# First dense block of a hybrid decoder layer, taken whole or in two halves of its inputs

## The chip, the cores and the metric

The kernel runs on one core of a Trainium2 chip. The metric is the device time of one execution in microseconds (us). Engines are named as in the profile: PE is TensorE's matmul, PEld its weight load, DVE is VectorE, ACT is ScalarE, POOL is GpSimd, SP is SyncE, which here issues the DMAs.

## What is computed

One layer of a conditioned decoder in float32, for a prompt of 2048 rows and for 64 sample rows, both 1024 wide. Cut to what matters here:

```
mod = silu(c) @ w_ada + b_ada               # 9 rows x 6144: sh1, sc1, gt1, sh2, sc2, gt2
h   = rms_norm(x, norm1_g) * (1 + sc1) + sh1
q, k, v, g, u, gate_r, gate_s = split(h @ w_in)
ret = retention(rotary(q), rotary(k), v);  ssm = s5(u)      # S5: a diagonal state space model
x   = x + gt1 * (merge of both branches by the gates) @ w_out
x   = x + gt2 * squared_relu_mlp(rms_norm(x) * (1 + sc2) + sh2)
```

The first four of the twelve 512-column pieces of `mod` are sh1 (pieces 0 and 1) and sc1 (pieces 2 and 3). Pieces 0 and 2 are all that the first 512 columns of h need, pieces 1 and 3 what the other 512 need.

## The kernel before

The prompt goes through the dense part in four super-blocks of 512 rows, and then through the feed-forward part. In a super-block, `block()` computes one 512-column piece of a dense product: u, q, k, v, g, four gate pieces, then glu, br, bs and wo. In the first super-block a further piece of the modulation (`ada4` to `ada11`) follows each of the first eight.

Float32 operands are split into a rounded high part and a rest, both of the type fp32r, and a product is three matmuls: high by high, high by rest, rest by high. The weights come as a stream of pieces of 256 rows by 512 columns (512 KB). `fetch` (line 181) loads one into a buffer `wraw` (four of them). `refill` splits it into `whi` on ACT (line 191) and `wlo` on POOL, or on DVE for the modulation's weights (line 194), and then fetches another. The split pieces lie in a ring of five. For block u four pieces (u in `for u in range(nu)`) of two 128-row steps each meet four groups of 128 output columns: 4 x 2 x 4 x 3 = 96 matmuls (line 253), which gather in four banks of PSUM. Pieces 0 and 1 meet only the first half of h (`hh[0]`, `hl[0]`), pieces 2 and 3 only the second (`hh[1]`, `hl[1]`).

`setup()` (from line 768) prepares the first super-block. It queues all loads on SP in this order: constants, the weights of modulation piece 0, the first two row blocks of x and the bias, the weights of piece 2, the other two row blocks, the weights of pieces 1 and 3, and four fetches of the stream. Then, for each half of the columns: the product of the shift piece (line 845), in the first half also the row norms of x on ACT and DVE (lines 639 to 644, 625 to 633, 860), the product of the scale piece, and for each of the four row blocks a turn on PE (line 852), scale and shift on DVE (`m`, line 685), the split into `hh` on ACT (line 687) and `hl` on POOL (line 688). So the products run in the order 0, 2, 1, 3. `mod_out` adds the bias (`mt`, line 878), turns the result (`ptm`, line 883) and copies it (line 884). Two refills stand between products 1 and 3, three more at the end.

`s5_setup` (from line 925) prepares the constants of S5, nearly all of it small operations on DVE, with loads on SP and some transposes on PE. It runs as a generator beside the blocks of the first super-block: `tick()`, called once for each piece and column group of a block, takes it a step further, and what is left after block k is written out at once (`finish`).

The order in the text is not the order on the engines. The context is built with `schedule_with_timeline_sim=True`: a planner lays the instructions of each engine's queue by a modelled timeline, and the engine then runs that queue as laid. `keep_in_program_order` (the refills of `setup`) pins an instruction behind what its engine was given before it. Tiles of one pool share its slots: 17 in the pool `units` for the large ones, and two PSUM pools of four banks each, `pd` for the blocks and `pm` for the rest.

Of the kernel before, what the change touches and what calls it, by code (L numbers as in the profile page):

```python
# [10 lines left out]
F32 = mybir.dt.float32  # L11
# [6 lines left out]
P = 128  # L18
# [7 lines left out]
RING, RAW = 5, 4  # L26
# [56 lines left out]
class Layer:  # L83
# [148 lines left out]
            del self.open_side[name]  # L232
            self.spawn(evac(st[0]))

    def block(self, name, kind, src, evac=None, sample=None, order="k"):
        nc = self.nc
        assert self.names[self.at] == name, (self.names[self.at], name)
        self.at += 1
        nu = 2 if name == "glu" or name[:2] in ("br", "bs") else 4
        nk = 2 * nu  # L240
        banks = [self.pd.tile([P, 512], F32, tag="pd", name=f"pd_{name}") for _ in range(4)] if kind else []
        sb = self.bank(f"ps_{name}", [P, 512]) if sample else None

        def products(k, j, w, kk):
            hi, lo = w
            xh, xl = src(k, j)
            if kind == "T":
                a = slice(j * P, j * P + P)
                mm = [(hi[:, kk, a], xh), (hi[:, kk, a], xl), (lo[:, kk, a], xh)]
            else:  # L250
                mm = [(xh, hi[:, kk]), (xh, lo[:, kk]), (xl, hi[:, kk])]
            for z, (a, b) in enumerate(mm):
                nc.tensor.matmul(banks[j], a, b, start=(k == 0 and z == 0), stop=(k == nk - 1 and z == 2))  # L253

        def sample_products(k, w, kk):
            st = sample[0](k)
            m = st.shape[-1]
            for z in range(2):
                nc.tensor.matmul(sb[:m], st, w[z][:, kk], start=(k == 0 and z == 0),
                                 stop=(k == nk - 1 and z == 1))  # L260

        if order == "k":
            for u in range(nu):
                w = self.weight(name)
                for j in range(4 if kind else 0):
                    for kk in range(2):
                        products(2 * u + kk, j, w, kk)
                    if u == nu - 1:
                        evac(j, banks[j])
                    if j == 0:  # L270
                        self.refills()
                    self.tick()
                if sample:
                    for kk in range(2):
                        sample_products(2 * u + kk, w, kk)
                    if u == nu - 1:
                        self.spawn(sample[1](sb))
                    if kind is None:
                        self.refills()
                        self.tick()  # L280
                self.due += 1
                self.side()
            return
        self.refills()
        ws = [self.weight(name) for u in range(nu)]
        for j in range(4):
            for u in range(nu):
                for kk in range(2):
                    products(2 * u + kk, j, ws[u], kk)
                if u == nu - 1:  # L290
                    evac(j, banks[j])
                self.tick()
                if j == 3 and not sample:
                    self.refill()
        if sample:
            for u in range(nu):
                for kk in range(2):
                    sample_products(2 * u + kk, ws[u], kk)
                self.tick()
                self.refill()  # L300
            return self.spawn(sample[1](sb))
# [466 lines left out]
    def setup(self):  # L768
# [28 lines left out]
        gn = self.work("gn", [16, P])  # L797
        dma(gn[0:8], i["norm1_g"].rearrange("o (k p) -> (o k) p", p=P))
        dma(gn[8:16], i["norm2_g"].rearrange("o (k p) -> (o k) p", p=P))
        wa = [self.unit("wa") for _ in range(8)]  # L800
        wv = i["w_ada"][0].rearrange("(k p) n -> p k n", p=P)

        def load(n):
            for a in range(2):
                dma(wa[2 * n + a], wv[:, 4 * a:4 * a + 4, 512 * n:512 * n + 512])

        xu = [self.unit("x0", shape=(P, 2, D)) for _ in range(2)]
# [5 lines left out]
        load(2)  # L813
        for j in range(2, 4):
            self.x_rows(xu[1][:, j - 2], 0, j)
        load(1)
        load(3)
        for _ in range(RAW):
            self.fetch()

        th = self.work("th", [9, D])
# [3 lines left out]
        pt = self.bank("pt", [P, 8, 9])  # L825
# [14 lines left out]
        x = [xu[j // 2][:, j % 2] for j in range(4)]  # L840

        def ada(n):
            pa = self.pd.tile([P, 512], F32, tag="pd", name=f"ps_ada{n}")
            for k in range(8):
                nc.tensor.matmul(pa[:9], z[:, k, 0:9], wa[2 * n + k // 4][:, k % 4], start=(k == 0), stop=(k == 7))
            self.mod_out(n, pa[0:9], ba[:, 512 * n:512 * n + 512])

        def turn(q, j):
            pt = self.bank("pt", [P, 4, P])
            for a in range(4):  # L850
                k = 4 * q + a
                nc.tensor.transpose(pt[:, a], x[j][:, k * P:k * P + P], self.ident)
            return pt

        for q in range(2):
            ada(q)
            if q == 0:
                for j in range(4):
                    r = self.now(self.row_rstd(x[j]))
                    V.tensor_scalar(x[j], x[j], r, None, op0=ALU.mult)  # L860
                pts = [turn(q, j) for j in range(4)]
            else:
                for _ in range(2):
                    self.refill(True)
            ada(2 + q)
            self.scales(2 + q)
            for j in range(4):
                pt = turn(q, j) if q else pts[j]
                self.norm_out(pt, q, self.s1[:, :, 0], self.modT[:, 0:8, 0], self.hh, self.hl, j, nc.gpsimd)
        for _ in range(RING - 2):  # L870
            self.refill(True)
        self.late_setup = self.s5_setup()
# [2 lines left out]
    def mod_out(self, n, p, bias):  # L875
        nc = self.nc
        t = self.work("mt", [9, 512])
        nc.vector.tensor_add(t, p, bias)
        if n in (4, 5, 10, 11):
            nc.sync.dma_start(self.modd[:, 512 * n:512 * n + 512], t)  # L880
        pt = self.pd.tile([P, 4, 9], F32, tag="pd", name="ptm")
        for a in range(4):
            nc.tensor.transpose(pt[:, a], t[:, a * P:a * P + P], self.ident[:9, :9])
        nc.vector.tensor_copy(self.modT[:, 4 * n:4 * n + 4], pt)
# [615 lines left out]
    def super_block(self, b, late):  # L1500
# [4 lines left out]
        hh, hl = self.hh, self.hl  # L1505
        srcT = lambda h, l: (lambda k, j: (h[k // 4][:, k % 4], l[k // 4][:, k % 4]))
# [8 lines left out]
        S = lambda st, ev: (lambda k: st[:, k], ev) if smp else None  # L1515
        hS = zS = None
        if smp:
            hS = self.hS
# [20 lines left out]
        nc.sync.dma_start(rot, self.i["rot"][b])  # L1539
        if b == 0:  # L1540
            s5 = self.spawn(self.late_setup, 2)
        self.block("u", "T", srcT(hh, hl), ev_u, S(hS, ev_us))
        if b:
            s5 = self.spawn(self.s5(b), 7)
        more_ada()
# [231 lines left out]
        order = "j" if b < NSB - 1 else "k"  # L1777
        self.block("wo0", "N", srcN(mh, ml), ev_wo(0), S(m2S, ev_woS(0)) if smp else None, order=order)
        f = self.block("wo1", "N", srcN(mh, ml), ev_wo(1), S(m2S, ev_woS(1)) if smp else None, order=order)
# [49 lines left out]
```

## Time and profile before

| | |
|---|---|
| median of 3 runs | 3114.01 us (3114.0 to 3119.35) |
| profiled execution | 3112.17 us |
| its span in the trace | 3110.3 us |
| busy share PE, DVE, POOL, ACT | 94%, 62%, 55%, 42% |
| mean granted TensorE clock | 0.965 |
| end of modulation product 3 | 57.99 us |
| block u on PE | 59.09 to 82.75 us |

Times are counted from the span's start. In a row of the timeline the first number is the start, the second the duration (of all where several are merged), then the engine, the line of the kernel, the operation, output and inputs, the count, and in brackets how long the engine had been idle and what released it. In a row of the groups, busy time and mean nanoseconds stand behind the count. In a row of the waits stand the total, how often, and the longest.

### The profile page before, as it was taken

The numbers are of one execution on the slowest core, as the hardware profiler recorded it, in microseconds if no ns is written. First come the engines' busy times: TensorE is split into PE (matmuls) and PEld (weight loads), VectorE is DVE, ScalarE is ACT, GpSimd is POOL, SyncE is SP. The second block draws the span as 40 slices with busy tenths as digits, with TensorE's granted clock in tenths as the row PEclk, the third lists the DMA queues.
The fourth block names the chain that finished last, engine by engine and source line by source line (L and its number), as shares of the span: only waits on it lengthen the run. The fifth ranks groups of instructions, "written<-read, shape, count | busy, mean of one in ns | idle before, by whom it ended". The sixth has DMA issues, their size and how long they took to land. (4 is left out here: it accounts for less than half of the span.)

```text
span 3110.3 us, 37430 instructions
## 1 busy us (share of the span) xinstructions
PE 2917.2 (94%) x13436; PEld 2381.2 (77%) x13436; DVE 1924.5 (62%) x3205; ACT 1319.7 (42%) x2060; POOL 1722.9 (55%) x1036
## 2 busy tenths in 40 slices
PE   7789999999998899999999989999999999998996
PEld 3567777888777778777788778887788788876885
DVE  5978675770576896467853556565555755554555
ACT  2232442222333234423234345556664555566643
POOL 2331464434354544556345576768778666688771
PEclk9889999999999899999899999999999999999998
DMA  8565445644345854458544455556545544466532
GB/s 226 157 194 204 133 129 150 180 123 118 83 121 164 263 172 123 138 141 250 183 129 152 147 198 174 197 180 210 182 156 181 195 163 149 153 217 224 188 129 95
DMA packets 336749, 518.62 MB, mean 167 GB/s; under 512 B 71462, under 2 KB 168246, under 8 KB 332459
## 3 DMA queue, kind: packets, MB, share of 16 engines
q1 hardware_dynamic: 336564, 516.23, 52.7%
q8 instruction: 106, 1.74, 0.2%
q14 instruction: 79, 0.65, 0.1%
HBM read 401.39 MB, written 114.78 MB: 166 GB/s over the span
## 5 line engine op out<-in xcount | busy, mean ns | idle before, releaser
L194 POOL TENSOR_TENSOR wlo<-wraw,whi 128x1024 fp32r<-128x1024 f32 x248 | 614.0, 2487 | 733.8 <-ACT whi L191 627.5
L191 ACT ACTIVATE whi<-wraw 128x1024 fp32r<-128x1024 f32 x312 | 324.5, 1057 | 629.8 <-PE pd_wo L253 61.8
L409 PE MATMUL pq_down<-shi,tw 128*128 128x512 f32 x1792 | 564.4, 394 | 20.6 <-DVE acc L469 9.8
L409 PE MATMUL pq_up<-shi,tw 128*128 128x512 f32 x1792 | 555.9, 390 | 12.8 <-ACT tw L310 7.1
L409 PEld LDWEIGHTS pq_down<-shi,tw 128*128 128x128 f32 x1792 | 338.9, 189 | 96.5 <-ACT acc L467 9.5
L409 PEld LDWEIGHTS pq_up<-shi,tw 128*128 128x128 f32 x1792 | 337.1, 188 | 85.7 <-ACT tw L310 8.3
L311 POOL TENSOR_TENSOR tw<-traw,tw 128x512 fp32r<-128x512 f32 x192 | 277.4, 1459 | 147.7 <-ACT tw L310 147.5
L409 PE MATMUL pq_down<-slo,tw 128*128 128x512 f32 x896 | 351.9, 393 | 0.9 <-DVE slo L382 0.9
L409 PE MATMUL pq_up<-slo,tw 128*128 128x512 f32 x896 | 349.1, 390 | 0.0
L469 DVE SCALAR_TENSOR_TENSOR acc<-pq_down,modT,acc 128x512 f32<-128x512 f32 x224 | 162.9, 746 | 108.6 <-PE pq_down L409 108.1
L396 ACT ACTIVATE shi<-sw 128x1024 fp32r<-128x1024 f32 x140 | 147.1, 1058 | 156.1 <-DMA sw<-sd 105.4
L409 PEld LDWEIGHTS pq_down<-slo,tw 128*128 128x128 f32 x896 | 169.8, 189 | 35.5 <-DVE slo L382 1.4
L409 PEld LDWEIGHTS pq_up<-slo,tw 128*128 128x128 f32 x896 | 168.7, 188 | 34.6
L382 DVE TENSOR_TENSOR slo<-sw,far 128x512 fp32r<-128x512 f32 x160 | 103.8, 683 | 115.1 <-ACT far L381 97.1
L310 ACT ACTIVATE tw<-traw 128x512 fp32r<-128x512 f32 x224 | 138.0, 625 | 55.7 <-PE pq_down L409 46.8
L419 ACT ACTIVATE aq<-pq_up 128x512 f32<-128x512 f32 x128 | 72.5, 592 | 191.0 <-PE pq_up L409 190.9
L401 DVE TENSOR_TENSOR slo<-sw,shi 128x1024 fp32r<-128x1024 f32 x60 | 105.7, 1781 | 66.9 <-ACT shi L396 63.2
L345 POOL TENSOR_TENSOR ts<-traw,ts 128x512 f32<-128x512 f32 x64 | 95.8, 1496 | 53.2 <-issue 50.5
L194 DVE TENSOR_TENSOR wlo<-wraw,whi 128x1024 fp32r<-128x1024 f32 x64 | 83.1, 1300 | 54.3 <-ACT whi L191 50.2
L310 ACT ACTIVATE tw<-ts 128x512 fp32r<-128x512 f32 x128 | 80.0, 626 | 86.0 <-PE pq_up L409 76.0
L345 POOL TENSOR_TENSOR ts<-traw 128x512 f32<-128x512 f32 x64 | 86.5, 1351 | 47.2 <-DMA traw<-in_w_up_dram 28.9
L447 DVE TENSOR_TENSOR sq<-aq 128x512 f32<-128x512 f32 x32 | 31.3, 979 | 131.0 <-ACT aq L424 131.0
(536 smaller groups left out, 6992.6 us busy)
## 6 DMA issues: line engine op xcount, KB each, us to landing
wraw<-in_w_in_dram SPq DMA_DIRECT2D x144, 512.0 KB
sw<-sd SPq DMA_DIRECT2D x112, 512.0 KB
s5p<-s5c SPq DMA_DIRECT2D x32, 1024.0 KB
traw<-in_w_up_dram SPq DMA_DIRECT2D x64, 512.0 KB
sd<-sq SPq DMA_DIRECT2D x32, 1024.0 KB
sd<-aq SPq DMA_DIRECT2D x32, 768.0 KB
traw<-in_w_down_dram SPq DMA_DIRECT2D x24, 1024.0 KB
wraw<-in_w_ada_dram SPq DMA_DIRECT2D x32, 512.0 KB
```

The lines of the kernel that those rows point to most:

```text
L191: a = nc.scalar.activation(hi, raw, AF.Copy)
L194: l = eng.tensor_sub(lo, raw, hi)
L310: self.nc.scalar.activation(t[:, 0], x, AF.Copy)
L311: eng.tensor_sub(t[:, 1], x, t[:, 0])
L345: G.tensor_sub(x[p], l, x[m] if isinstance(m, int) else m)
L382: self.nc.vector.tensor_sub(d, a, c)
L396: nc.scalar.activation(hi[:, a], t, AF.Copy)
L401: V.tensor_sub(lo[:, a], t, hi[:, a])
L409: self.nc.tensor.matmul(bank, w, x, start=(first and a == 0 and z == 0), stop=(a == 3 and z == 2), skip_group_check=True)
L419: copy = lambda d, b: nc.scalar.activation(d, b, AF.Copy)
L447: V.tensor_add(S[:, 0], A21, A22)
L469: V.scalar_tensor_tensor(d, b, g, d, op0=ALU.mult, op1=ALU.add)
```

## The change

`block()` gets a parameter `part`. With part 0 it takes only the first two pieces of u's weights and keeps the four banks; with part 1 it goes on in these banks with the other two, and only then are the results taken out. Part 0 is called in `setup()` at the end of the first half of the columns: between product 2 with its norm, and product 1. Part 1 stands where the whole block stood, in the first super-block alone; the others call the block whole.

The loads change their order: two fetches of the weight stream now come ahead of the weights of products 1 and 3, the other two behind them. Those weights and the last two fetches stand behind product 0 in the text. The two pinned refills move to the end of the first half of the columns. Since u holds all banks of `pd` from part 0 on, products 1 and 3 and their turned results take banks of `pm`. The tiles for the modulation weights are allocated when they are loaded, no longer all ahead.

```
-    def block(self, name, kind, src, evac=None, sample=None, order="k"):
+    def block(self, name, kind, src, evac=None, sample=None, order="k", part=None):
...
-        self.at += 1
+        if part != 0:
+            self.at += 1
...
-        banks = [self.pd.tile([P, 512], F32, tag="pd", name=f"pd_{name}") for _ in range(4)] if kind else []
+        if part == 1:
+            banks = self.held
+        else:
+            banks = [self.pd.tile([P, 512], F32, tag="pd", name=f"pd_{name}") for _ in range(4)] if kind else []
+            self.held = banks
...
-            for u in range(nu):
+            for u in range(nu) if part is None else range(2 * part, 2 * part + 2):
...
-        wa = [self.unit("wa") for _ in range(8)]
+        wa = {}
...
             for a in range(2):
+                wa[2 * n + a] = self.unit("wa")
                 dma(wa[2 * n + a], wv[:, 4 * a:4 * a + 4, 512 * n:512 * n + 512])
...
-        load(1)
-        load(3)
-        for _ in range(RAW):
+        for _ in range(2):
             self.fetch()
...
-            pa = self.pd.tile([P, 512], F32, tag="pd", name=f"ps_ada{n}")
+            pa = self.pm.tile([P, 512], F32, tag="pm", name=f"ps_ada{n}") if n % 2 else \
+                self.pd.tile([P, 512], F32, tag="pd", name=f"ps_ada{n}")
...
             ada(q)
             if q == 0:
+                load(1)
+                load(3)
+                for _ in range(RAW - 2):
+                    self.fetch()
                 for j in range(4):
...
-            else:
-                for _ in range(2):
-                    self.refill(True)
             ada(2 + q)
...
+            if q == 0:
+                for _ in range(2):
+                    self.refill(True)
+                hh, hl = self.hh, self.hl
+                self.block("u", "T", lambda k, j: (hh[k // 4][:, k % 4], hl[k // 4][:, k % 4]), part=0)
...
-        pt = self.pd.tile([P, 4, 9], F32, tag="pd", name="ptm")
+        pool = ("pm", self.pm) if n % 2 else ("pd", self.pd)
+        pt = pool[1].tile([P, 4, 9], F32, tag=pool[0], name="ptm")
...
-        self.block("u", "T", srcT(hh, hl), ev_u, S(hS, ev_us))
+        self.block("u", "T", srcT(hh, hl), ev_u, S(hS, ev_us), part=None if b else 1)
```

## The prediction

> **What bounds the kernel now.** First the page, its totals and its slices.
>
> ```profile
> span 3110.3 us, 37430 instructions
> PE 2917.2 (94%) x13436; PEld 2381.2 (77%) x13436; DVE 1924.5 (62%) x3205; ACT 1319.7 (42%) x2060; POOL 1722.9 (55%) x1036
> PE   7789999999998899999999989999999999998996
> DVE  5978675770576896467853556565555755554555
> ```
>
> PE is busy for 94% of the span, so it sets the length over the whole. The exception is the first three slices (78 us each), the only early stretch where its digit falls to 7 and 8, and the change lies in the first. There I read the windows.
>
> ```profile
> 9.86:59.09 49.23, 38.66 (x112) 10.70 (x112) 18.69 (x66) 10.00 (x23) 9.69 (x6) 0.93 0.89 253
> 30.00:40.00 10.00, 6.18 (x22) 1.88 (x21) 5.34 (x25) 2.67 (x8) 0.00 (x0) 0.88 0.96 295
> 50.00:60.00 10.00, 9.22 (x32) 3.17 (x33) 1.98 (x7) 2.47 (x3) 6.54 (x4) 1.00 0.66 221
> 59.09:82.75 23.66, 23.66 (x108) 18.95 (x107) 22.90 (x77) 11.04 (x15) 9.84 (x6) 1.00 0.77 170
> 82.75:207.00 124.25, 94.37 (x419) 72.95 (x418) 121.91 (x243) 33.68 (x41) 47.43 (x21) 0.89 0.52 166
> ```
>
> The columns are the stretch, its length, then busy time of PE, PEld, DVE, ACT and POOL, the granted clock, the DMA share and GB/s. Until 59 us the DMA engines are busy for 0.89 and PE idles 49.23 - 38.66 = 10.6 us. Block u runs from 59.09 to 82.75 with PE full. Then, until 207 us, DVE is full (121.91 of 124.25) and PE idles 29.9 us. The waits from 60 to 260 us name who holds PE:
>
> ```profile
> PE pd_k L253 <- DVE rt L1553: 10.2, 1, 10.2
> PE pw L1151 <- DVE s5bx L1144: 8.0, 1, 8.0
> PE pt L909 <- DVE mt L903: 7.7, 1, 7.7
> PE pd_v L253 <- DVE rt L1553: 3.6, 1, 3.6
> ```
>
> All four are DVE. It works through the S5 setup from about 65 us, so from u on what counts is when DVE's stream starts and how fast it runs, not when PE finishes u. The timeline shows how that start comes about.
>
> ```profile
> 24.38 8.47 PE L845 MATMUL ps_ada<-wa,z 128*9 128x512 f32 x16 [4.43 <-DMA wa<-in_w_ada_dram]
> 38.32 8.32 PE L845 MATMUL ps_ada<-wa,z 128*9 128x512 f32 x16 [2.15 <-DMA wa<-in_w_ada_dram]
> 43.97 0.75 DVE L860 TENSOR_SCALAR x<-x,y 128x1024 f32<-128x1024 f32 x1
> 46.57 1.97 PE L852 MATMUL pt<-cpk,x 128*128 128x128 f32 x16
> 50.95 7.04 PE L845 MATMUL ps_ada<-wa,z 128*9 128x512 f32 x16
> 59.09 0.50 PE L253 MATMUL pd_u<-hh,whi 128*128 128x512 f32 x1
> 59.95 5.21 DVE L685 TENSOR_SCALAR m<-pt,s,modT 128x128 f32<-128x128 f32 x16
> 62.07 5.13 POOL L688 TENSOR_TENSOR hl<-m,hh 128x512 fp32r<-128x512 f32 x4 [5.54 <-ACT hh L687]
> 65.06 0.90 DVE L978 TENSOR_SCALAR s5w<-s5w 128x32 f32<-128x32 f32 x1
> 65.20 0.63 ACT L687 ACTIVATE hh<-m 128x512 fp32r<-128x512 f32 x1 [0.65 <-DVE m L685]
> 67.17 4.75 POOL L194 TENSOR_TENSOR wlo<-wraw,whi 128x1024 fp32r<-128x1024 f32 x2
> 82.75 0.39 PE L259 MATMUL ps_ada<-whi,cT 128*41 128x512 f32 x1
> ```
>
> The modulation products run in the order 0, 2, 1, 3 (24.38 is product 2, 38.32 product 1, 50.95 product 3, which ends at 57.99). Product 3 releases the second norm half: DVE 59.95 to 65.16, last hh at 65.83, last hl at 67.20. Today the first half of u already runs under that work, which is the cover that the change takes away.
>
> **The change part by part.** Every operation is kept; 48 of u's 96 products, two weight loads and two weight splits move. What it costs depends on three arrivals.
>
> ```profile
> 18.11 15.70 SPq L805 DMA_DIRECT2D wa<-in_w_ada_dram  x4
> 33.85 7.81 SPq L181 DMA_DIRECT2D wraw<-in_w_in_dram  x4
> 41.19 2.54 POOL L688 TENSOR_TENSOR hl<-m,hh 128x512 fp32r<-128x512 f32 x2 [40.75 <-ACT hh L687]
> 51.88 4.65 POOL L194 TENSOR_TENSOR wlo<-wraw,whi 128x1024 fp32r<-128x1024 f32 x2
> 54.27 2.67 SPq L181 DMA_DIRECT2D wraw<-in_w_ada_dram  x2
> 58.88 0.42 SPq L944 DMA_DIRECT2D s5w<-in_ssm_log_dt_dram  x1
> ```
>
> (a) SP. Two weight pieces (512 KB each, 1.05 MB) move ahead of the four 1 MB loads for products 1 and 3. At the 295 GB/s of the 30 to 40 us row that is 3.6 us: product 1 starts at about 38.3 + 3.6 = 41.9 instead of 38.32. By the row of the whole stretch (253 GB/s) it is 4.2 us. It ends 8.25 us later, at 50.1.
>
> (b) When the half block can start. The fourth row block of x is scaled at 44.7 (43.97 + 0.75). A turn is a third of the 1.97 us burst (0.7), the four DVE operations are a quarter of 5.21 (1.3), hh takes 0.63, hl half of 2.54 (1.3) and the pinned first wlo half of 4.65 (2.3). That gives 44.7 + 0.7 + 1.3 + 0.6 + 1.3 + 2.3 = 50.9. So the half block cannot fill the gap in front of product 1; PE gets to it after product 1, at 50.1 to 50.9.
>
> (c) PE. Half of 23.66 us is at most 11.8; 96 products without the setup's transposes between them are nearer 22, so 11.0. The half block runs from 51 to 62. It stands ahead of product 3 in the program, so product 3 runs from 62 to 69: the release of the second norm half moves by 69.0 - 58.0 = +11.0 us. It is bounded by +3.6 (product 3 goes first, only the loads are late) and +20 (the half block goes before product 1 too).
>
> (d) DVE in the meantime. The raw buffers of the first two pieces now come free after wlo at 51 and 53.2 rather than 54.2 and 56.5, so the small S5 loads behind those fetches on SP are issued some 3 us earlier than 58.88. DVE then has the chain for dt to do, which needs nothing from product 3, in time that was idle (the 50 to 60 us row: DVE 1.98 of 10):
>
> ```profile
> L980 DVE CAST s5w<-s5w 128x32 int32<-128x32 f32 x1 | 2.3, 2326 | 0.0
> L981 DVE CAST s5w<-s5w 128x32 f32<-128x32 int32 x1 | 2.3, 2312 | 0.0
> L986 DVE SCALAR_TENSOR_TENSOR s5w<-s5w 128x32 f32<-128x32 f32 x11 | 2.0, 183 | 0.2
> L979 DVE TENSOR_SCALAR s5w<-s5w 128x32 f32<-128x32 f32 x1 | 1.3, 1258 | 0.0
> L978 DVE TENSOR_SCALAR s5w<-s5w 128x32 f32<-128x32 f32 x1 | 0.9, 895 | 0.0
> ```
>
> These are 2.3 + 2.3 + 2.0 + 1.3 + 0.9 = 8.8 us; seven more of this shape at 0.183 make it 10.1. Between 57 and 71 us all of it fits. But POOL's splits stand beside DVE here: operations of 0.18 us take 2.3 in 67.17 to 71.9. One such split (the fourth piece) still comes behind hl and will hold some other operation for 2.4 us. The credit is 10.1 - 2.4 = 7.7, bounded by 0 (the order written for DVE has the norm first, so DVE waits) and 10.1.
>
> [...]
>
> (e) PE behind u. The second half needs the last hh, which trails product 3 by 65.83 - 57.99 = 7.8 us. So it runs from 76.8 to 88.6, 5.9 us later than 82.75, after a gap of 7.8 us. What such a gap costs more is seen after the wait for L903:
>
> ```profile
> 101.83 0.59 PE L909 MATMUL pt<-cpk,mt 9*128 9x9 f32 x4 [7.69 <-DVE mt L903]
> 102.36 1.22 PE L253 MATMUL pd_q<-hh,wlo 128*128 128x512 f32 x2
> 105.88 0.40 PE L253 MATMUL pd_q<-hl,whi 128*128 128x512 f32 x1
> ```
>
> Eight products took 3.52 us, 0.44 each against 0.23 (22 us by 96): +1.7. PE is late by 7.6 us, and that same wait of 7.7 us covers it. If the cover is gone, the sum is +7.6. [...]
>
> (f) The rest. Products 1 and 3 take banks of the second pool, since u now holds all four of the first; the transposes of the second half then queue behind product 3. One is 0.7 us, and 1.9 us of mt, ptm and scales (57.99 to 59.95) run over it: 0, bounded by 2.6 for four. If slots are reused in the order they were taken, those of x and not of wa now come first, so the loads of the S5 matrices on SP may wait for these transposes; SP's fetches queue behind, and the weights in the ring feed PE meanwhile: 0, bounded by +4. Eight fewer ticks under u leave more of the setup for later: an order, no work, bounded by 3.6 either way (the smallest of the four waits).
>
> Sum: +11.0 - 7.7 = +3.3 us. The profiled execution took 3112.17 us (its span and 1.9 around it); the median is 3114.01. So 3115.5 against the profile, 3117.3 against the median.
>
> **The rivals.** *Product 3 first* (faster): the plan puts product 3 straight after product 1, at 50.1, and ends it at 57.1 to 58 because the turns now lie in the gap before product 1. The half block covers the norm as today, and dt's credit stays: -7.7, 3106.3. For it: its loads land early (issued by 33.8 today). Against: the half block stands first in the program and is nearly ready at 50. *Half block first* (slower): the plan puts it ahead of product 1 too. It waits for the hl and wlo chain until 51 whatever the loads do, ends at 62, product 1 at 70.3, product 3 and its hand-over at 78.3: +20.3 - 7.7 = +12.6, 3126.6. This decides once the plan has x ready before the loads of product 1. For it: program order, and the loads now come later. Against: in today's order the plan placed product 1 ahead of the last turns. *No change in effect*: product 3 keeps its place and DVE's order keeps the norm first; only part of the 3.6 us shows: +0 to +3.6, some 3115.8.
>
> **How the numbers follow.** Forecast 0.40, product 3 first 0.25, half block first 0.20, no effect 0.15. This kernel's measurements can tell 0.2%, 6.2 us, from no change. The forecast's own range is +0.9 to +11 (a credit of 10.1 at one end, none at the other); I put a quarter of it over +6.2, since the rows speak for a credit near 7.7. Slower: 0.20 + 0.10 = 0.30. Faster: 0.25. Within: 0.30 + 0.15 = 0.45. The range 3104 to 3128 holds the three priced cases with a little beyond the fast one.
>
> **What would show it.** (a) Product 1 starting at 41 to 43. (b, c) pd_u products in two groups, the first from about 51 to 62 between products 1 and 3, and product 3 ending near 69. (d) L978 before the second group of L685. (e) A PE gap of some 7 us in front of the second group, and the wait for L903 nearly gone; DVE still full until about 210. The forecast is wrong if product 3 ends before 60, if the half block starts before 45, or if DVE is not the engine that holds PE at 200 us.

## The result and the profile after

The changed kernel takes 3142.31 us (median of 6 runs, 3138.3 to 3145.8) against 3119.29 us of the kernel before measured beside it (6 runs, 3114.0 to 3126.75): a ratio of 1.0079, 95% interval 1.0061 to 1.0097. It is slower by some 24 us; the forecast was +3.3. Runs of the kernel before spread by 13 to 36 us between the lowest and the highest of a batch, so the times of the experiments come from several runs each. A place is read from one profile, and places scatter too. Two kernels below, e14 and e16, have the order of before on every engine until after the start of the S5 setup. Their product 1 starts at 40.6 and 41.9 us instead of 38.3, their first S5 operation at 66.1 and 68.7 instead of 65.1. In e16:

```profile
41.88 8.34 PE L845 MATMUL ps_ada<-wa,z 128*9 128x512 f32 x16 [2.13 <-DMA wa<-in_w_ada_dram]
```

So a difference of less than some 4 us between the places of two kernels says little by itself.

The totals of the page after, and its slices:

```profile
span 3144.0 us, 37436 instructions
PE 2928.8 (93%) x13436; PEld 2391.6 (76%) x13436; DVE 1925.6 (61%) x3205; ACT 1319.0 (42%) x2060; POOL 1717.6 (55%) x1036
PE   6779998999998889999899989999999999998996
DVE  3997755682484896376863455655656855554555
```

The work is the same (DVE 1925.6 us busy against 1924.5). DVE's first slice falls from 5 to 3, so DVE has lost time at the very start. The windows of after say where (columns as in the prediction):

```profile
50.00:80.00 30.00, 27.82 (x105) 14.04 (x103) 4.94 (x15) 3.95 (x6) 8.92 (x5) 0.98 0.60 133
82.43:235.00 152.57, 117.32 (x510) 92.13 (x510) 147.91 (x309) 42.84 (x55) 50.24 (x24) 0.86 0.47 151
```

The same two windows of before:

```profile
50.00:80.00 30.00, 29.22 (x122) 19.17 (x123) 21.51 (x69) 11.10 (x15) 16.38 (x10) 1.00 0.73 175
65.06:213.90 148.84, 118.96 (x536) 93.86 (x535) 143.33 (x310) 44.61 (x57) 54.29 (x25) 0.89 0.54 167
```

From 50 to 80 us DVE worked 4.94 us instead of 21.51. The second row of each fence runs from DVE's first operation on the dt chain to the end of the last `pw` transpose of the S5 setup on PE; I call it the S5 stream. It starts 17.4 us later (82.43 against 65.06), is 3.7 us longer and ends 21.1 us later (235.0 against 213.9). Those 21 us are still there at the end of the block glu (439.6 against 417.8), and they are the loss. The two profiled executions differ by another 12 us behind glu (2692.6 and 2704.4 us); the other kernels below, all with the same work there, take from 2684.4 (e12) to 2704.8 us (e10), so I count that as scatter.

The timeline of after shows why the stream starts late (lines of the changed kernel: L850 is the product, L895 `ptm`, L690 `m`, L990 the first operation of the dt chain):

```profile
47.19 1.09 PE L857 MATMUL pt<-cpk,x 128*128 128x128 f32 x4 [6.61 <-DVE x L869]
48.20 8.53 PE L850 MATMUL ps_ada<-wa,z 128*9 128x512 f32 x16
56.66 1.21 PE L258 MATMUL pd_u<-hh,whi 128*128 128x512 f32 x4
56.77 0.68 DVE L889 TENSOR_TENSOR mt<-ps_ada,ba 9x512 f32<-9x512 f32 x1 [7.09 <-PE ps_ada L850]
67.81 0.41 PE L895 MATMUL ptm<-cpk,mt 9*128 9x9 f32 x4
68.15 7.04 PE L850 MATMUL ps_ada<-wa,z 128*9 128x512 f32 x16
68.25 0.33 SPq L953 DMA_DIRECT2D lam<-in_ssm_lambda_re_dram  x1
70.02 0.42 SPq L956 DMA_DIRECT2D s5w<-in_ssm_log_dt_dram  x1
77.19 5.20 DVE L690 TENSOR_SCALAR m<-pt,s,modT 128x128 f32<-128x128 f32 x16
82.43 0.72 DVE L990 TENSOR_SCALAR s5w<-s5w 128x32 f32<-128x32 f32 x1
83.10 1.22 PE L258 MATMUL pd_u<-hh,whi 128*128 128x512 f32 x2 [4.17 <-ACT hh L692]
```

Product 1 stands behind the last turn of x, which itself waited 6.61 us for DVE. The half block follows from 56.66 to 67.8. The turn of product 1's result (`ptm`) is in PE's queue behind the half block, though its input `mt` was there at 57.45. Product 3 comes last, 68.15 to 75.19. The waits of after from 60 to 260 us, on PE, and one on SP's queue:

```profile
PE pd_v L258 <- DVE rt L1565: 8.7, 1, 8.7
PE pw L1163 <- DVE s5bx L1156: 8.0, 1, 8.0
PE pd_k L258 <- DVE rt L1565: 7.9, 1, 7.9
PE pt L921 <- DVE mt L915: 6.3, 1, 6.3
PE pd_u L258 <- ACT hh L692: 4.2, 1, 4.2
SPq L953 <- PE ptm L895: 9.1, 1, 9.1
```

The four long ones are still DVE's. On SP the small load for lambda waits 9.1 us for `ptm`: by the kernel's text its work tile takes over a buffer that `mt` of product 1 held, and `ptm` is that tile's last reader.

### The profile page after: what moved, and what is told of

It is laid out like the page before. It is cut to its first block, busy times and chain, and to the rows that moved or that the text cites. A ratio compares the mean times of both kernels' runs of the same rounds, so it can differ in the third digit from the quotient of the medians.

```text
span 3144.0 us, 37436 instructions
## 1 busy us (share of the span) xinstructions
PE 2928.8 (93%) x13436; PEld 2391.6 (76%) x13436; DVE 1925.6 (61%) x3205; ACT 1319.0 (42%) x2060; POOL 1717.6 (55%) x1036
## 4 chain that ended last, share of the span: by engine, by line
PE 68%; DVE 15%; DMA 7%; issue 3%; POOL 3%; ACT 2%; SPq 1%; DVEq 0%; ACTq 0%; POOLq 0%
PE pq_up L414 17%; PE pq_down L414 12%; PE pd_gr L258 5%; PE pd_gs L258 5%; PE pd_wo L258 3%; PE pd_g L258 3%; PE pd_u L258 2%; PE pd_br L258 2%; DMA sw<-sd 2%; PE pd_q L258 2%; PE pd_v L258 1%; PE pd_glu L258 1%; DMA gt<-modd 1%; PE pd_k L258 1%; PE pd_bs L258 1%
## 5 line engine op out<-in xcount | busy, mean ns | idle before, releaser
L191 ACT ACTIVATE whi<-wraw 128x1024 fp32r<-128x1024 f32 x312 | 323.4, 1056 | 635.4 <-PE pd_wo L258 65.1
L258 PE MATMUL pd_wo<-whi,mh 128*128 128x512 f32 x256 | 101.9, 402 | 14.5 <-DVE tw L1727 14.5
L316 POOL TENSOR_TENSOR tw<-t,tw 128x512 fp32r<-128x512 f32 x64 | 91.5, 1434 | 43.5 <-ACT tw L315 43.4
```

The lines of the kernel that those rows point to most:

```text
L191: a = nc.scalar.activation(hi, raw, AF.Copy)
L316: eng.tensor_sub(t[:, 1], x, t[:, 0])
```

## The experiments

Theory S: the time follows the S5 stream on DVE, as the prediction has it, and after is slow because the stream starts late and is longer. Its rivals: the loads' new order costs the time (L), PE's late block u does (E), or taking the block in two parts does, wherever the first part stands (P). Later came theory T, on the steps of the setup. The table has the places from each profile in us, and the change against before from the ratio (95% interval in brackets).

| kernel | product 1 starts | product 3 ends | stream starts | last pw ends | against before, us |
|---|---|---|---|---|---|
| before | 38.3 | 58.0 | 65.1 | 213.9 | |
| after | 48.2 | 75.2 | 82.4 | 235.0 | +24.6 [+19.0, +30.3] |
| e1 | 41.4 | 62.5 | 69.5 | 219.3 | +5.0 [-0.9, +11.2] |
| e2 | 52.3 | 73.5 | 85.7 | 234.9 | +13.4 [+6.9, +20.3] |
| e3 | 50.3 | 78.2 | 85.4 | 239.0 | +17.2 [+10.0, +24.3] |
| e4 | 49.5 | 77.2 | 84.4 | 237.8 | +16.5 [+10.3, +22.8] |
| e5 | 57.7 | 81.9 | 67.8 | 222.2 | +0.9 [-4.4, +6.2] |
| e6 | 37.8 | 64.3 | 58.7 | 216.4 | +14.6 [+8.7, +20.2] |
| e7 | 52.8 | 70.3 | 88.4 | 237.9 | +25.5 [+17.1, +33.9] |
| e8 | 42.4 | 61.0 | 68.1 | 225.4 | +14.0 [+8.7, +19.3] |
| e9 | 50.9 | 67.1 | 74.3 | 230.1 | +16.5 [+10.3, +22.7] |
| e10 | 46.1 | 67.0 | (7.3) | 221.4 | +13.1 [+8.7, +17.4] |
| e11 | 54.9 | 82.5 | (7.4) | 220.2 | +3.7 [-1.2, +8.4] |
| e12 | 46.3 | 65.1 | 72.2 | 219.8 | +0.9 [-4.0, +6.2] |
| e13 | 47.4 | 75.2 | 82.5 | 225.2 | +19.3 [+13.7, +25.2] |
| e14 | 40.6 | 59.0 | 66.1 | 223.3 | +10.3 [+5.9, +15.0] |
| e15 | 54.1 | 81.2 | (7.3) | 224.4 | +12.2 [+6.2, +17.8] |
| e16 | 41.9 | 61.6 | 68.7 | 215.4 | +2.2 [-3.4, +7.8] |
| e17 | 43.4 | 62.4 | 79.9 | 230.5 | +25.8 [+19.0, +32.7] |
| e18 | 43.0 | 64.0 | 81.5 | 228.4 | +16.8 [+10.6, +23.0] |

**The loads: e1_loads_only and e4_old_loads.** e1 is before with two fetches ahead of the weights of products 1 and 3; e4 is after with the old order.

```
e1, on before                     e4, on after
+        for _ in range(2):       +        load(1)
+            self.fetch()         +        load(3)
         load(1)                  -        for _ in range(2):
         load(3)                  +        for _ in range(RAW):
-        for _ in range(RAW):                  self.fetch()
+        for _ in range(RAW - 2):
             self.fetch()         (and not again behind product 0)
```

> The kernel before with one part of the change alone: two fetches of the weight stream ahead of the loads for products 1 and 3. Theory S (the change costs what it delays the S5 setup's start on DVE, 65.06 before and 82.30 after, +17.2 us): the loads delay product 1 by 3.6 us at most, so DVE's start moves by 0 to 4 us and the time by 0 to +4 us against before. Rival L (the order of the loads is the cause, since product 1 starts at 48.2 instead of 38.3): +10 us or more against before.

> The changed kernel with the order of the loads of before; the half block stays between products 2 and 1. Theory S: if the plan puts product 1 ahead of the last turn again (it waited for it until 48.2), product 3 ends some 8 us earlier and the time is +12 to +17 against before; if not, +23 as changed. Rival L: the loads were the cause, so within 5 us of before.

e1 started product 1 at 41.4, where the prediction's term (a) had 41.9, and costs about 5 us, with an interval that reaches just below zero. e4 still has product 1 at 49.5 and the stream at 84.4. So the loads' order is at most a small part of the loss, about a fifth by its middle value and not told from nothing, and L falls. The time of e4 lies 8 us below that of after, but the two intervals overlap, and its median is 22.4 us above that of before.

**Where lambda's tile lies: e3_lam_in_z.** After, with lambda in spare columns of the tile of silu(c), so that its load waits for no `mt`.

```
-        lam = self.work("lam", [G, 4, 64])
+        lam = self.zu[0:G, 512:768].rearrange("g (a n) -> g a n", a=4)
```

> The changed kernel with the S5 input lam in spare columns of the tile z instead of a work tile, so that its load, and the loads behind it on SP, no longer wait for the transposes of product 1's result (67.8). Theory S with the reason that the credit of step (d) failed for this buffer: the loads come 10 us or more earlier, the chain for dt runs in DVE's idle time before the second norm half, and the time falls by 5 to 10 us under the changed kernel (+13 to +18 against before). Rival E (what sets the end is PE's own lateness: block u ends at 97.9 instead of 82.9): unchanged, +23.

The loads of lambda went out at 43.8 to 48, but the load of the time step still came at 61.2, behind the three fetches, and DVE's queue still had the second half's rows ahead of the dt chain. The stream started at 85.4. The 9.1 us wait on SP is real, but no gain from taking it away alone is shown: the stream starts and ends no earlier than in after, and the time, though lower by the ratio, has an interval that overlaps with after's (by the medians it is +22.9).

**The head of the setup early: e5_after_s5_early and e6_before_s5_early.** All that needs only lambda and the time step is written ahead of the half block (e5), or in before ahead of product 1 (e6); lambda lies as in e3. The loads and transposes of the S5 matrices b and c come behind this head.

```
             if q == 0:
+                self.late_setup = self.s5_setup()
+                while next(self.late_setup) != "head":
+                    pass
```

> The changed kernel with the head of the S5 setup (the loads of its four smallest inputs and every operation that needs only those, about a quarter of its DVE stream) put ahead of the half block in the text, with the tile z lending space as in the run with lam in z. On PE nothing moves: the half block still stands before product 3 and block u still ends some 15 us late. Theory S (the time follows the start of the S5 stream on DVE): DVE does the head between 50 and 75 us, where it was idle, and the time falls by 12 to 20 us under the changed kernel, to 0 to +10 us against before. Rival E (the lateness of PE and of block u sets the time): no gain, +15 to +23.

> The kernel before with the same head of the S5 setup put ahead of product 1 in the text; nothing else is changed. Theory S: DVE is idle for some 8 us between 51 and 60, so the stream gains 5 to 10 us and the time falls by as much, -5 to -10 against before. Rival E: PE's order is untouched, 0.

e5 gets the whole loss back, though every product is later than in after. Its waits (first row) and timeline:

```profile
DVE s5w L978 <- DMA s5w<-in_ssm_log_dt_dram: 15.6, 1, 15.6
```

```profile
57.74 7.34 PE L851 MATMUL ps_ada<-wa,z 128*9 128x512 f32 x16
67.76 0.18 DVE L978 TENSOR_SCALAR s5w<-s5w 128x32 f32<-128x32 f32 x1 [15.63 <-DMA s5w<-in_ssm_log_dt_dram]
74.82 3.60 PE L851 MATMUL ps_ada<-wa,z 128*9 128x512 f32 x8
86.21 5.20 DVE L690 TENSOR_SCALAR m<-pt,s,modT 128x128 f32<-128x128 f32 x16
```

The second half's rows come at 86.21 (77.19 in after) and u ends at 106.0 (97.9 in after, 82.9 in before), yet the kernel is at +0.9. That refutes E: PE may be 23 us late with u and the time does not follow. The stream begins at 67.76, and its first operation takes 0.18 us where before's took 0.90. e6 was a miss. The head has a transpose of lambda on PE, which stands ahead of the last turns, `ptm` and product 3 and waits there for lambda's load:

```profile
52.67 0.28 PE L957 MATMUL pl<-cpk,z 32*128 32x32 f32 x1 [5.12 <-DMA z<-in_ssm_lambda_re_dram]
```

So product 3 ends at 64.3, 6.3 us later than in before, and the second half's rows, now with S5 operations between them on DVE, end at 73.3 instead of 65.2. The two kernels also show that the end of the last `pw` orders times only roughly: it comes 8.3 us later than in before in e5, which costs nothing that can be measured, and 2.5 us later in e6, which costs 14.6 us. Part of this is the one profile: that of e6 (3117.2 us) is 7 us below its median.

**The half block put back: e2_half_behind_3, e7_half_pinned, e9_pinned_behind_turns, e8_pinned_old_banks.** All four are after with the half block called behind product 3. In e2 the planner may still move it. In e7 it is pinned behind product 3's `ptm`, in e9 behind the second half's turns too. e8 is e7 with products 1, 3 and their `ptm` in the banks of `pd`, as before.

```
e2          e7                                        e9
 ada(3)      ada(3)                                    ada(3)
+block u,0  +with tc.issue_after(last ptm of 3):      +turns of the second half
            +    block u, part 0                      +with tc.issue_after(last turn):
                                                      +    block u, part 0
e8, on e7
-            pa = self.pm.tile(...) if n % 2 else self.pd.tile(...)
+            pa = self.pd.tile([P, 512], F32, tag="pd", name=f"ps_ada{n}")
                                          (and the tile of ptm likewise)
```

> The changed kernel with the half block moved behind product 3, all else as in the change (loads, banks, tiles). Theory S: product 3 ends before 62, the half block covers the second norm half as in the kernel before, the S5 stream starts by 70, and the time is that of before within 6 us, so some 20 us under the changed kernel. Rival L: the loads are still late, +10 us or more against before. Rival P (what costs is the block being taken in two parts and its banks and ticks, wherever the first part stands): no better than the changed kernel, about +23 us.

> The changed kernel with the half block pinned behind product 3's turned result on PE; loads and the second PSUM pool for products 1 and 3 stay as in the change. Theory S: product 1 still waits for the last turn (48), product 3 ends near 65, the S5 stream starts at 72 to 75, +6 to +12 against before. Rival P (block in two parts, whatever the place): +15 or more.

> The kernel after, with the first half of the u block held back until product 3, its transposes and the second half's four turns of x have been issued on TensorE; loads and banks stay those of after. Theory S (the time follows the S5 setup stream on VectorE, and that starts behind the last modulated row of the second half): product 1 still comes behind the last turn of the first half, at about 48 to 52 us, product 3 ends at 65 to 70, the stream starts at 72 to 78 (65.1 before, 82.4 after), and the kernel is 8 to 15 us slower than before, less than after. Theory B (the two pm banks and the ticks cost the time, not the place of the half block): as slow as after, +21 to +23. Theory E (TensorE's late products of u set it): u ends at about 100 to 106, so slower than after.

> As the pinned run, with products 1 and 3 and their turned results back in the first PSUM pool, which is free until the pinned half block starts. In its plan product 1 is again ahead of the last turn. Theory S with the second pool as the reason for product 1's late start: product 3 ends at 60 to 63, the S5 stream starts at 67 to 72, the time is +2 to +8 against before, like the run with the loads alone (+5). Rival P: +15 or more. If the pool does not matter: as the pinned run.

e2 and e7 are no clean return. In e2 the planner laid much of the half block ahead of product 3, which starts at 66.45, and the rest ahead of its `ptm` at 78.86. In e7 the turns of the second half came behind the half block, at 82.4. In e9 and e8 they did not, and up to product 1 these two differ in the banks alone. Product 1 in e9, with `pm`, then in e8, with `pd`:

```profile
50.89 8.11 PE L850 MATMUL ps_ada<-wa,z 128*9 128x512 f32 x16
42.40 8.53 PE L849 MATMUL ps_ada<-wa,z 128*9 128x512 f32 x16 [1.40 <-DMA wa<-in_w_ada_dram]
```

In e9 it follows the fourth turn, in e8 it stands ahead of it and waits for its load alone. The stream starts at 74.3 and at 68.1. The kernel e12 below, with the order of e8 up to there, has 46.3 and 72.2, so the banks move the stream's start by 2.1 to 6.2 us; the two times (+16.5 and +14.0) are too close to show it. What did not fit theory S: in e8 the stream starts only 3.0 us later than in before, and the kernel is 14 us slower. Its stream takes 157.3 us instead of 148.8. At this point e7 (+25.5) and e8 (+14.0) lay nearer to rival P than to S.

**The missing steps: e12_pinned_ticks, e13_after_ticks, e14_before_fewer_ticks.** `block()` calls `tick()` once for each piece and column group, and each call takes the S5 setup further. The half block makes eight of these calls before the setup is spawned, so they are lost. e12 is e8, and e13 is after, with eight calls given back; e14 is before with eight calls left out and nothing else changed.

```
e12, e13                                       e14
 s5 = self.spawn(self.late_setup, 2)            s5 = self.spawn(self.late_setup, 2)
+for _ in range(8):                            +self.mute = 8     # the next 8 ticks return
+    self.tick()
```

> The kernel after with product 1, product 3 and their transposes back in the banks of before and the half block held back behind product 3's transposes (e8: +14 us, of which only 3 us are a later start of the S5 stream), and eight more steps of the S5 setup given right behind its spawn, as many as the half block took from it. If the missing steps made the stream longer in e8: the stream is back at about 149 us, and the kernel at +3 to +7. If something else did: +12 to +16 as e8.

> The kernel after, with one edit: eight steps of the S5 setup are given right behind its spawn, as many as the half block took from it (its ticks fall before the setup exists). Theory T (the loss of after has two parts: the S5 stream starts 17 us late, and the eight steps fewer make it some 8 to 10 us longer): the stream still starts at about 82 us, is some 146 to 149 us long instead of 152.6, ends at 228 to 231 instead of 235, and the kernel is at +11 to +16 instead of +21 to +29. Theory L (only the late start counts, the steps matter only in the pinned kernels): it stays within 4 us of after.

> The kernel before, with one edit: the first eight steps that block u would give the S5 setup are left out, so the setup begins eight products groups later in the plan, as in after. Nothing of the half block is moved. Theory T: the stream starts at about 65 us as in before, but ends 7 to 11 us later (221 to 225 instead of 213.9), and the kernel is 7 to 12 us slower than before. Theory L: within 3.6 us of before, the bound of the prediction.

All three came out on the side of T. e12 is at +0.9 where e8 was at +14.0, with a stream of 147.6 us instead of 157.3. That ends rival P, since in e12 too the block is taken in two parts. e14 makes before alone 10.3 us slower, with the stream starting 1.0 us later and ending 9.4 us later. e13 ends the stream 9.8 us earlier than after, from the same start; its time fell by less than I expected, to +19.3 (expected +11 to +16, which its interval reaches). The window over the stream of e14:

```profile
66.06:223.30 157.24, 120.99 (x536) 94.22 (x534) 148.68 (x310) 44.02 (x56) 53.32 (x25) 0.87 0.51 159
```

And over that of e13:

```profile
82.46:225.20 142.74, 115.78 (x510) 90.37 (x510) 138.21 (x309) 42.43 (x55) 59.21 (x24) 0.88 0.44 145
```

The same 309 operations keep DVE busy for 147.91 us in after and for 138.21 in e13. So the steps do not add work; the same operations take longer. The timeline of before shows them undisturbed:

```profile
113.73 0.68 DVE L1139 TENSOR_TENSOR s5bx<-s5bc,s5pw 128x512 f32<-128x512 f32 x1
115.07 0.69 DVE L1141 TENSOR_TENSOR s5pk<-s5bc,s5pw 128x512 f32<-128x512 f32 x1
119.75 2.42 POOL L194 TENSOR_TENSOR wlo<-wraw,whi 128x1024 fp32r<-128x1024 f32 x1 [24.36 <-PE pw L1151]
120.19 0.69 DVE L1552 TENSOR_TENSOR rt<-pd_q,rot 64x512 f32<-64x512 f32 x1
```

The timeline of e14 has them beside POOL's splits:

```profile
122.54 11.11 POOL L197 TENSOR_TENSOR wlo<-wraw,whi 128x1024 fp32r<-128x1024 f32 x4
123.05 2.86 DVE L1144 TENSOR_TENSOR s5pk<-s5bc,s5pw 128x512 f32<-128x512 f32 x1
125.83 2.85 DVE L1145 TENSOR_TENSOR s5bx<-s5bc,s5pw 128x512 f32<-128x512 f32 x1
```

So has that of after:

```profile
134.64 11.13 POOL L194 TENSOR_TENSOR wlo<-wraw,whi 128x1024 fp32r<-128x1024 f32 x4
135.16 2.85 DVE L1153 TENSOR_TENSOR s5pk<-s5bc,s5pw 128x512 f32<-128x512 f32 x1
137.94 2.85 DVE L1154 TENSOR_TENSOR s5bx<-s5bc,s5pw 128x512 f32<-128x512 f32 x1
140.71 2.86 DVE L1151 TENSOR_TENSOR s5bx<-s5bc,s5pw 128x512 f32<-128x512 f32 x1
143.50 2.82 DVE L1152 TENSOR_TENSOR s5bx<-s5bc,s5pw 128x512 f32<-128x512 f32 x1
```

In e13 the first of them come in time:

```profile
129.21 0.69 DVE L1151 TENSOR_TENSOR s5bx<-s5bc,s5pw 128x512 f32<-128x512 f32 x1
```

A product of two 128x512 tiles takes 0.69 us by itself and 2.85 beside a split on POOL. With its eight steps the setup has reached these products before POOL's splits go on in block q; without them they fall on four splits in a row. The operations that read `s5bc`, nearly all of them such products, show what this is worth. DVE's busy time in them over the stream, in after and then in e13:

```profile
82.43:235.00 152.57, 42.57 (x38) 0.86 0.47 151
82.46:225.20 142.74, 33.31 (x38) 0.88 0.44 145
```

These 9.3 us are nearly all of the 9.7 us by which DVE's busy time differs. The same 38 operations take 42.6 us in e14 against 36.6 in before, and 42.6 in e8 against 36.2 in e12.

**Ways to beat both kernels: e10_before_s5_first, e11_after_s5_first, e15_after_s5_first_ticks, e16_before_more_ticks.** e10 and e11 load lambda and the time step at the very top of SP's queue and give the head to DVE from 7.3 us on; e15 is e11 with eight steps more, e16 is before with eight steps more. As in e5, what belongs to the matrices b and c comes behind the head.

```
e10, e11 (in setup, ahead of all loads)         e15, e16: the loop of e13
+        self.late_setup = self.s5_setup()
+        next(self.late_setup)                  # its loads of lambda and time step
```

> The kernel before, with the loads of the S5 block's lambda and time step at the very top of SP's queue and the operations that need only those (the head of the setup) given to VectorE ahead of product 0's result or right behind product 1's. Theory S: the head, some 10 us of VectorE, lies in the idle time ahead of product 0 and beside product 1, nothing of the modulation is delayed, the stream behind the last row of the second half gets shorter by 8 to 12 us, and the kernel is 8 to 20 us faster than before. Rival: the stream's end is set by its waits on the other engines (the splits on GpSimd, the transfers of b and c), then 0 to -3 us.

> The kernel after, with the same head of the S5 setup first. Theory S: the rest of the stream starts while TensorE makes the half block, so the loss of after (+21 to +23) goes: between 5 us faster and 5 us slower than before. Theory E (TensorE's late products set it): it stays at +15 or more, since product 3 and u end as late as in after.

> The kernel after with the head of the S5 setup first (+4.7 us against before) and the eight steps given back. Theory T: the rest of the stream gets shorter by 5 to 10 us, last pw at 210 to 215 instead of 220.2, so 0 to 6 us faster than before. Theory L: unchanged, +3 to +7.

> The kernel before with eight more steps given to the S5 setup behind its spawn. Theory T, if more steps go on helping: the stream ends 3 to 8 us earlier than 213.9 and the kernel is 3 to 8 us faster than before. If before already gives enough of them: within 3 us of before.

None beats the kernel before. e11 stays within its expectation and below after by some 20 us, like e5. e10 was a miss, and its timeline shows the reason:

```profile
46.09 6.35 PE L848 MATMUL ps_ada<-wa,z 128*9 128x512 f32 x8 [4.55 <-DMA wa<-in_w_ada_dram]
59.98 7.03 PE L848 MATMUL ps_ada<-wa,z 128*9 128x512 f32 x16
72.15 0.67 DVE L883 TENSOR_TENSOR mt<-ps_ada,ba 9x512 f32<-9x512 f32 x1
72.88 0.59 PE L888 MATMUL ptm<-cpk,mt 9*128 9x9 f32 x4 [5.86 <-DVE mt L883]
```

Product 1 starts 7.8 us later than in before, and product 3's result, there at 67.01, waits 5.1 us for DVE, which works through the setup first. e15 was a miss too: eight steps more made e11 slower by about 8 us, so more steps are not better as such. The operations on `s5bc` take 36.2 us of DVE in it against 33.2 in e11; the rest of the 8 us is not explained. e16 changes nothing that can be measured, and its profile says why: these operations fall to 26.7 us from 36.6 in before, but DVE is busy over the stream for 143.1 us as against 143.3. Others lose as much, among them those on `s5w` (48.3 us instead of 43.1); that they now stand beside the splits is inferred.

**Product 1 ahead of the fourth turn: e17_product1_first and e18_product1_first_ticks.** After, with product 1 and its `ptm` written between the third and the fourth turn of the first half, so that its bank is taken first; e18 has the eight steps as well.

```
-                pts = [turn(q, j) for j in range(4)]
+                pts = [turn(q, j) for j in range(3)]
             ada(2 + q)
             self.scales(2 + q)
+            if q == 0:
+                ada(1)
+                pts.append(turn(q, 3))
             (and ada(q) at the head of the loop for q == 0 alone)
```

> The kernel after, with product 1 and what belongs to it written ahead of the fourth turn of the first half, so that its bank of the second pool is taken before that turn's. Theory B (the bank's place in the order is what makes product 1 late in after): product 1 runs at 41 to 50 us instead of 48.2 to 56.7, and what hangs on it is 5 to 7 us earlier: the last row of the second half at 75 to 78 instead of 82.4, the S5 stream starts with it, and the kernel is 4 to 7 us faster than after, so +15 to +19 against before. Rival: product 1 waits for its load or for x as long as in after, and nothing changes.

> The same with the eight steps of the S5 setup given back. If the two causes add (the bank's place some 6 us, the steps some 8 to 10): +6 to +10 against before, what is left being the half block's own 11 us ahead of the second half's row. If the prediction's credit for the dt chain came too: 0 to +4.

Product 1 moved to 43.4, as expected, and the time did not follow: a miss. The timeline of e17:

```profile
43.36 8.72 PE L850 MATMUL ps_ada<-wa,z 128*9 128x512 f32 x16 [1.51 <-DMA wa<-in_w_ada_dram]
52.72 3.90 DVE L690 TENSOR_SCALAR m<-pt,s,modT 128x128 f32<-128x128 f32 x12
55.40 7.04 PE L850 MATMUL ps_ada<-wa,z 128*9 128x512 f32 x16 [0.62 <-DVE m L690]
73.47 0.41 PE L898 MATMUL ptm<-cpk,mt 9*128 9x9 f32 x4
```

DVE's queue now had `mt` of product 1 ahead of the first half's rows, so these came at 52.72 instead of 40.0 and the half block at 62.4 instead of 56.7. Product 3 ended at 62.4, ahead of the half block, but its `ptm` stood behind it, at 73.47. The stream started 2.5 us earlier than in after and no more. e18 lies 9 us below e17, though the intervals overlap, and its stream is 3.7 us shorter; at +16.8 it missed its +6 to +10 as well.

## Why the prediction was wrong

The bound it named was right in the main. The S5 stream on DVE sets the time of this stretch: e5 starts it early with everything on PE late, and the loss goes. The sum was +11.0 - 7.7 = +3.3; the profiles have +17.4 - 6.1 + 9.8 = +21.1 at the end of the stream (a later start, a stream that is shorter by itself, and the missing steps). Two of the terms that failed had been put at nothing: the banks and the steps.

- **(a) fits in size, its price is not shown.** Product 1 comes 17.3 us behind the start of product 2 with the loads moved alone (e1), and 13.6 to 14.2 us in before, e14 and e16: 3.1 to 3.7 us later, forecast 3.6. This is one profile, and e10, which has the old order behind some small loads, has 17.4 too. That e1 has it at 41.4 as forecast is partly luck, since e16 has 41.9 with the old order. In time it is +5.0 in e1 with an interval that reaches below zero, and e12, which has the new order too, is at +0.9.
- **(b), (c) right in kind, 6.2 us too small.** The half block ran between products 1 and 3 and took 11.15 us (forecast 11.0), but from 56.7 and not from 51, so product 3 ended at 75.2 and not at 69.0. The half block waited for product 1, which ended at 56.7 and not at 50.1.
- **(f), banks: the first step that failed.** It was priced at 0, bounded by 2.6, for the turns behind product 3. What the second pool did was to put product 1 behind the four turns of the first half: 48.2 instead of 41.9. That it does so because product 1 takes its bank of `pm` after them is inferred; e17, where it is written ahead of the fourth turn, has it at 43.4. The prediction itself had quoted that before places product 1 ahead of the last turn, and did not ask whether that survives the change of pool. e8 and e12 against e9 show it, by 2.1 to 6.2 us of the stream's start. What it is worth in time alone was not isolated: in e17 the first half's rows moved with it.
- **(d) failed as put, with a credit of nearly the same size in another place.** The dt chain did not go into DVE's idle time: its loads came at 70.0 and not 3 us before 58.88, behind a wait of 9.1 us for `ptm`, which stood behind the half block; and even with lambda's tile moved (e3) the order on DVE had the rows first. That is the lower end of the term's own bound, 0. The gain that came is that the late stream is shorter by itself: 142.74 us in e13, from the same start as in after, against 148.84 in before. Of these 6.1 us, 1.9 lie ahead of the first 512-column product (46.75 us from 82.46 to 129.21, against 48.67 from 65.06 to 113.73), where POOL is busy for 13.8 us instead of 18.3 beside the small operations. The operations on `s5bc` give 3.3 (33.3 against 36.6); the rest is open.
- **(e) wrong in size, rightly priced at nothing.** u ended at 97.9, 15 us late, and not 5.9; the gap ahead of its second half is 4.17 us and not 7.8. The wait for `mt` behind it did not vanish (6.3 against 7.7), since DVE is late as well. e5 shows that PE's lateness is covered.
- **(f), eight steps fewer: the second step that failed.** "An order, no work, bounded by 3.6 either way", taken at 0. It is no work, but it decides what runs beside POOL's splits, and it makes the stream 8.4 us longer in before (e14), 9.8 in after against e13, and 9.6 in e8 against e12. In before that is 10.3 us of time. The bound had been taken from the smallest wait of PE, a row that has nothing to do with the mechanism; the row that has was quoted for (d), an operation of 0.18 us that takes 2.3 beside a split.

Of the rivals, "half block first" came nearest in its course: product 3 at 78.3 and +12.6. Its place was wrong, as product 1 ran ahead of the half block. With the half block behind product 3, the old banks and the steps given back (e12), +0.9 [-4.0, +6.2] of the +24.6 is left, so these three edits together undo the loss. For the steps alone the price is shown (e14, and e8 against e12). The place of the half block and the banks were only undone together: with the steps given back, they are the difference between e13 (+19.3) and e12.

Two readings in the prediction were off without effect on its sum: the burst of 16 transposes is four turns and not three, and product 1's row has 8.32 us and not 8.25.

## What to carry to other kernels

When work is moved in a planned kernel, ask of each helper that counts calls, of each tile pool and of each buffer that is reused who now stands behind whom: the first two decided here, the third held up the S5 loads, and only the moved matmuls had been costed fully. An order that adds no work can still cost if two engines disturb each other (here 2.85 us instead of 0.69 for a product, and 10.3 us of time in e14), so its bound comes from the slowed rows and their number, not from a wait. And an engine that looks busiest in the profile may run 23 us late in one stage at no measurable cost (e5), while one that seems idle there sets the time.

## What the runs showed of the hardware that I had not expected

The size of DVE's slowdown beside POOL, and an operation that showed none. Two inputs of 128x512 in SBUF take 0.69 us alone (115.07 in before) and 2.85 beside a split of 2.78 (11.13 by 4), one for one. A cast of 128x32 takes 0.18 us in e5 without a split beside it and 2.33 in before with one (L980 in both), so the short operation pays as much as the long one, some 2.15 us. At 120.19 in before the product `rt<-pd_q,rot` (64x512), with one input in PSUM, takes 0.69 beside a split that runs from 119.75 to 122.17. These rows do not show what decides whether an operation is slowed. One after the other, a split and a product would take 2.42 + 0.69 = 3.11 us, an estimate from the split at 119.75 and the product alone. In the four rows of after each product starts 2.77 to 2.79 us behind the last, so a pair is close to one after the other, but not exactly that.
